# Choice of experts in a two-block transformer kernel: lists in their own place, ten U tiles kept back, more rows gathered early, angles at the end

## The chip, the cores and the metric

The kernel runs on one core of one Trainium2 chip. The metric is the device time of one launch in microseconds. Before the change the median of 3 runs is 2347.88 us (2346.62 to 2350.38).

## The reference

512 tokens of width 1024 go through two blocks. The part that the change touches is the feed-forward of the first block, a choice among 16384 experts (PEER). For each token, each of 8 heads scores two sets of 128 keys, takes the 16 best of each, adds them up in pairs, and takes the 16 best of the sums. These name 128 experts a token; expert i has a row of expert_u and a row of expert_v.

```
q = (xb @ w_q).reshape(p, PEER_HEADS, 2, PEER_DK_HALF)
sc = jnp.einsum('phcd,hcnd->phcn', q, sub_keys)
top_s, top_i = lax.top_k(sc, PEER_TOPK)
cand_s = top_s[:, :, 0, :, None] + top_s[:, :, 1, None, :]      # reshaped to (p, heads, 256)
cand_i = top_i[:, :, 0, :, None] * N_KEYS + top_i[:, :, 1, None, :]
best_s, best_pos = lax.top_k(cand_s, PEER_TOPK)
idx = jnp.take_along_axis(cand_i, best_pos, axis=-1)
g = jax.nn.softmax(best_s, axis=-1)
act = jax.nn.gelu(jnp.einsum('phkd,pd->phk', expert_u[idx], xb), approximate=False)
return jnp.einsum('phk,phkd->pd', g * act, expert_v[idx])
```

The second block (attention with rotary angles, then SwiGLU) needs cos and sin of the positions; they are computed inside the first block and put aside in DRAM (`csd`).

## The kernel before

The first block's mixer runs to about 245 us, PEER to about 1560, the second block to the end. Every fp32 weight is split in two parts, `whi` by ScalarE and `wlo` by VectorE or POOL (`split`, L91), and each product takes three matmuls.

Of the 512 tokens, 384 (three tiles) are done densely. All 16384 rows of expert_u are gone through as 128 tiles of U (`u_step(e)`, 24 matmuls and a Gelu each). The activations of the first 66 go to DRAM (`actd`), those of the next 22 stay in a ring. Their gates form a matrix G, built from one-hot tiles `oj`, `oi`, `oa` on VectorE (L813 to L816) and 48 product groups of 16 matmuls on TensorE (`pg`, L826 and L828), copied by ScalarE to `stage`, and written by SyncE to `gdram`. Then come 128 `v_step(e)`: read the activation, multiply by G (`cf`, L901), split (`ch`, `cl`), 18 matmuls with a tile of V. U steps 88 to 127 run beside V steps 66 to 105; this is called the middle stage. G comes in loads of eight steps (L899), U and V in blocks of two tiles (`raw`, L97), all through SyncE's queue.

The fourth tile of 128 tokens gathers: POOL fetches a row of expert_u for each token (`gather`, L641) and VectorE takes its dot product (L655, called a row), 128 times; then a Gelu, and 128 rows of expert_v, added up (L668). This tile is chosen first, so its rows can start early. `gs` is the generator of these steps.

`topk` (L482) is the choice for one tile on VectorE: MAX8, index and replace on 16 lists of 128 scores, then the candidates. The scores of the first tile are evicted during the w_q projection, those of the others go to DRAM (`scd`) and come back through SyncE.

What sets the order: `chain()` yields the VectorE work in pieces with a cost each, added to `now`. While `pe`, the work given to TensorE, is behind `now`, a U step is put in (4.2 each, 28 at the start); products are put in 9 after their one-hots; every 7 of cost a row. Within the v steps rows are spread by stage weights. A scheduler then fixes the order of each engine; each engine works in its order and waits where data is missing.

Of the kernel before, what the change touches and what calls it, by code (L numbers as in the profile page):

```python
# [18 lines left out]
P = 128  # L19
T = 512  # L20
# [6 lines left out]
U_PE = 4.2  # L27
G_PE = 1.8
LO_DVE = 1.25
ROW_DVE = 1.3  # L30
LAG = 9.0
U_LATE = 28.0
G_EVERY = 7.0
ROWS_AHEAD = 2
# [5 lines left out]
TB = 16  # L40
# [14 lines left out]
STARTS = [sum(ROWS[:a]) for a in range(16)]  # L55
# [13 lines left out]
class K:  # L69
# [412 lines left out]
    def topk(self, sc, tkp, consts, res, after_scores):  # L482


        nc = self.nc
        stc, wtc, btc = consts
        s1 = tkp.tile([P, 16, 16], F32, name="s1")
        ix = tkp.tile([P, 16, 16], U32, name="ix")
        for lo in (0, 8):
            for hc in range(16):  # L490
                nc.vector.max(s1[:, hc, lo:lo + 8], sc[:, hc])
                if hc % 4 == 3:
                    yield 1.1, True
            for hc in range(16):
                nc.vector.max_index(ix[:, hc, lo:lo + 8], s1[:, hc, lo:lo + 8], sc[:, hc])  # L495
                if hc % 4 == 3:
                    yield 1.4, True
            if lo == 0:
                for hc in range(16):
                    nc.vector.match_replace(out=sc[:, hc], in_to_replace=s1[:, hc, 0:8], in_values=sc[:, hc],  # L500
                                            imm_value=NEG)
                    if hc % 4 == 3:
                        yield 1.4, True
        after_scores()
# [11 lines left out]
        for lo in (0, 8):  # L516
            for h in range(8):
                nc.vector.max(bv[:, h, lo:lo + 8], cand[:, h])
            yield 1.5, True
            for h in range(8):  # L520
                nc.vector.max_index(bp[:, h, lo:lo + 8], bv[:, h, lo:lo + 8], cand[:, h])
            yield 2.1, True
            if lo == 0:
                for h in range(8):
                    nc.vector.match_replace(out=cand[:, h], in_to_replace=bv[:, h, 0:8], in_values=cand[:, h],
                                            imm_value=NEG)
                yield 2.1, False

# [57 lines left out]
    def peer(self):  # L586
# [3 lines left out]
        with ExitStack() as ctx:  # L590
# [54 lines left out]
            def gsteps():  # L645
                rows = []
                for k in range(P + ROWS_AHEAD):
# [28 lines left out]
            sctx = ctx.enter_context(ExitStack())  # L676
            scp = self.pool("sc", 1, ctx=sctx)

            def score_tile():
                return scp.tile([P, 16, P], F32, name="sc")  # L680

            order = list(reversed(range(T // P)))
            sc = [score_tile()]
            with ExitStack() as pctx:
# [32 lines left out]
                posi = tr[:, 0].bitcast(I32)  # L717
                nc.sync.dma_start(posi, a["pos"].to_broadcast([P, T]))
                nc.vector.tensor_copy(tr[:, 1], posi)
                hpi = kp.tile([P, 1], F32, name="hpi")  # L720
                nc.vector.memset(hpi, float(np.pi / 2))
# [9 lines left out]
            with ExitStack() as pctx:  # L731
                rp.append(self.pool("ring", 1, None, rctx, "right"))
                stgp = self.pool("stg", 2, ctx=pctx)
                ohp = self.pool("oh", 4, ctx=pctx)
                kp = self.pool("pk", 1, ctx=pctx)
                tkp = self.pool("tk", 1, ctx=pctx)
# [4 lines left out]
                stc = kp.tile([P, 16, 4], F16, name="stc")  # L741
                wtc = kp.tile([P, 16, 4], F16, name="wtc")
                btc = kp.tile([P, 16, 4], F16, name="btc")
                for r in range(16):
                    nc.gpsimd.memset(stc[:, r], float(STARTS[r]))
                    nc.gpsimd.memset(wtc[:, r], float(STARTS[r] - STARTS[r - 1]) if r else 0.0)
                    nc.gpsimd.memset(btc[:, r], float(r))
                io32 = kp.tile([P, P], I32, name="io32")
                nc.gpsimd.iota(io32, pattern=[[1, P]], base=0, channel_multiplier=0)
                iota4 = kp.tile([P, P, 4], F16, name="iota4")  # L750
                nc.vector.tensor_copy(iota4, io32[:, :, None].to_broadcast([P, P, 4]))
                consts = (stc, wtc, btc)

# [39 lines left out]
                def gates(tt):  # L793
# [13 lines left out]
                    for n in range(P // 8):  # L807
# [10 lines left out]
                        def products(n=n, oj=oj, oi=oi, oa=oa):  # L818
                            b, half = divmod(n, 2)
                            if half == 0:  # L820
                                stage[b] = stgp.tile([P, P, TB], F32, name="stage")
                            first = None
# [25 lines left out]
                self.early = -1  # L848
                dve = 0.0

                def pace(single):
                    while pe[0] < now[0] and todo:
                        u_step(todo.pop(0), nc.gpsimd if single else nc.vector)
                        pe[0] += U_PE
                        if not single:
                            now[0] += LO_DVE

                owed = [0.0]

                for cost, single in chain():  # L860
                    now[0] += cost
                    drain()
                    pace(single)
                    if self.early >= 0:
                        owed[0] += cost
                        while owed[0] > G_EVERY and self.early < P:
                            owed[0] -= G_EVERY
                            next(gs)
                            self.early += 1
                            now[0] += ROW_DVE  # L870
                while queue or todo:
                    now[0] += 1.0
                    drain(not todo)
                    pace(False)
                    owed[0] += 1.0
                    while owed[0] > G_EVERY and self.early < P:
                        owed[0] -= G_EVERY
                        next(gs)
                        self.early += 1
                        now[0] += ROW_DVE  # L880
            sctx.close()
# [684 lines left out]
```

## Time and profile before

| | us |
|---|---|
| median of 3 runs | 2347.88 |
| the profiled execution | 2345.79 |
| its span | 2344.0 |
| TensorE busy | 2204.4 (94%) |
| VectorE busy | 1652.3 (70%) |
| ScalarE busy | 921.5 (39%) |
| POOL busy | 533.9 (23%) |

The share of busy time is a mean over stages with different limits. In the chain of work that ended last TensorE has 75%, VectorE 14% and transfers 6%. A row of the trace gives start, duration, engine, line, operation, output and inputs, and in brackets how long the engine was idle before and what ended it. A time stretch of a window row is in us from the start of the span.

### The profile page before, as it was taken

Reading aid. Unit: us, or ns where it says so; the run is one execution under the profiler, and the core shown is the slowest. Engines: PE = TensorE matmul, PEld = TensorE weight load, DVE = VectorE, ACT = ScalarE, POOL = GpSimd, SP = SyncE. Lnnn points to the kernel's source line nnn. Section 1 sums busy time; section 2 is a strip of 40 time slices with the busy share of each in tenths; the row PEclk is TensorE's granted clock in tenths of the full one; section 3 lists DMA queues with packets and bytes.
Section 4 is the critical chain, followed back from the end, with each engine's and each line's share of the span. In section 5 each row is a group of like instructions: output and inputs, shape, how many; then the busy total and the mean of one; then the engine's idle time right before and its main releaser. Section 6 shows DMA issues by size and latency. Waiting matters only on the chain.

```text
span 2344.0 us, 29873 instructions
## 1 busy us (share of the span) xinstructions
PE 2204.4 (94%) x11063; PEld 1909.1 (81%) x11063; DVE 1652.3 (70%) x3113; ACT 921.5 (39%) x1345; POOL 533.9 (23%) x458
## 2 busy tenths in 40 slices
PE   4999989799999789999799999999999999999998
PEld 4888788699999768788688888878777888888887
DVE  8785679999777466778788887976666665444423
ACT  3623443246465423333233333354444554333321
POOL 3010022503300212333555554420112100000000
PEclk9989999999999989999899999999999999999999
DMA  7482344766766789999989998952221253322222
GB/s 277 147 283 75 135 170 165 256 220 249 251 231 223 268 280 314 324 314 336 330 319 345 345 351 323 320 169 100 81 69 55 97 173 117 108 90 96 82 91 74
DMA packets 158307, 483.66 MB, mean 206 GB/s; under 512 B 12232, under 2 KB 80456, under 8 KB 128080
## 3 DMA queue, kind: packets, MB, share of 16 engines
q1 hardware_dynamic: 116688, 330.73, 40.3%
q0 software_dynamic: 41472, 151.01, 18.2%
q8 instruction: 87, 1.43, 0.3%
q14 instruction: 60, 0.49, 0.1%
HBM read 429.65 MB, written 52.05 MB: 206 GB/s over the span
## 4 chain that ended last, share of the span: by engine, by line
PE 75%; DVE 14%; DMA 6%; issue 3%; ACT 1%; POOL 0%; SPq 0%; DVEq 0%; POOLq 0%; ACTq 0%
PE mm L115 12%; PE mm L117 12%; PE mm L118 12%; PE po L115 5%; PE act L118 5%; PE act L115 5%; PE act L117 5%; PE po L117 5%; PE po L118 5%; DMA sp<-actd 5%; DVE row L655 2%; PE pg L826 2%; PE pg L828 2%; DVE wlo L93 1%; DVE ix L495 1%
## 5 line engine op out<-in xcount | busy, mean ns | idle before, releaser
L93 DVE TENSOR_TENSOR wlo<-raw,whi 128x1024 fp32r<-128x1024 f32 (+1 forms) x380 | 454.4, 1201 | 260.4 <-ACT whi L92 256.1
L92 ACT ACTIVATE whi<-raw 128x1024 fp32r<-128x1024 f32 (+1 forms) x415 | 427.5, 1036 | 494.3 <-PE mm L117 196.1
L117 PE MATMUL mm<-hl,whi 128*128 128x512 f32 x928 | 368.9, 398 | 4.3 <-DVE hl L318 2.2
L115 PE MATMUL mm<-hh,whi 128*128 128x512 f32 x928 | 367.9, 400 | 4.5 <-ACT hh L471 1.6
L118 PE MATMUL act<-hh,wlo 128*128 128x384 f32 x1024 | 349.4, 342 | 17.0 <-DVE wlo L93 13.2
L118 PE MATMUL mm<-hh,wlo 128*128 128x512 f32 x928 | 363.8, 397 | 0.0
L115 PE MATMUL act<-hh,whi 128*128 128x384 f32 x1024 | 349.7, 342 | 2.7 <-ACT sp L612 2.7
L117 PE MATMUL act<-hl,whi 128*128 128x384 f32 x1024 | 348.5, 340 | 0.0
L115 PE MATMUL po<-whi,ch 128*128 128x512 f32 x768 | 268.6, 396 | 46.6 <-ACT ch L92 23.3
L117 PE MATMUL po<-wlo,ch 128*128 128x512 f32 x768 | 302.3, 394 | 4.4 <-DVE wlo L93 4.3
L118 PE MATMUL po<-whi,cl 128*128 128x512 f32 x768 | 296.1, 391 | 0.0
L641 POOL DMA_INDIRECT row<-in_eu_dram,gidx x128 | 171.2, 1337 | 531.6 <-DVE row L655 439.3
L641 POOL DMA_INDIRECT row<-in_ev_dram,gidx x128 | 184.4, 1441 | 184.9 <-DVE acc L668 146.8
L117 PEld LDWEIGHTS mm<-hl,whi 128*128 128x128 f32 x928 | 178.1, 192 | 43.0 <-DVE hl L972 3.0
L118 PEld LDWEIGHTS act<-hh,wlo 128*128 128x128 f32 x1024 | 195.2, 191 | 21.1 <-DVE wlo L93 15.6
L115 PEld LDWEIGHTS mm<-hh,whi 128*128 128x128 f32 x928 | 177.2, 192 | 42.6 <-ACT hh L471 2.0
L115 PEld LDWEIGHTS po<-whi,ch 128*128 128x128 f32 x768 | 145.4, 190 | 78.5 <-ACT whi L92 25.2
L118 PEld LDWEIGHTS mm<-hh,wlo 128*128 128x128 f32 x928 | 177.6, 191 | 37.1 <-DVE wlo L93 0.3
L115 PEld LDWEIGHTS act<-hh,whi 128*128 128x128 f32 x1024 | 195.7, 191 | 6.2 <-ACT sp L612 3.7
L117 PEld LDWEIGHTS act<-hl,whi 128*128 128x128 f32 x1024 | 195.6, 191 | 1.8
L92 ACT ACTIVATE ch<-cf 128x384 fp32r<-128x384 f32 x128 | 67.0, 525 | 325.1 <-PE po L117 167.1
L117 PEld LDWEIGHTS po<-wlo,ch 128*128 128x128 f32 x768 | 145.6, 190 | 36.2 <-DVE wlo L93 6.8
(476 smaller groups left out, 3444.3 us busy)
## 6 DMA issues: line engine op xcount, KB each, us to landing
raw<-in_uT_dram SPq DMA_DIRECT2D x64, 1024.0 KB
raw<-in_v_dram SPq DMA_DIRECT2D x64, 1024.0 KB
raw<-in_w_in_dram SPq DMA_DIRECT2D x26, 1024.0 KB
gdram<-stage SPq DMA_DIRECT2D x24, 1024.0 KB
G<-gdram SPq DMA_DIRECT2D x16, 1536.0 KB
raw<-in_w_gu_dram SPq DMA_DIRECT2D x22, 1024.0 KB
actd<-sp SPq DMA_DIRECT2D x66, 192.0 KB
sp<-actd SPq DMA_DIRECT2D x66, 192.0 KB
```

What stands on the lines that cost most here:

```text
L92: self.nc.scalar.activation(hi, src, AF.Copy)
L93: (eng or self.nc.vector).tensor_tensor(lo, src, hi.bitcast(F32), op=ALU.subtract)
L115: ins = nc.tensor.matmul(out, wh, xh, start=start and i == 0, stop=False)
L117: nc.tensor.matmul(out, wh, xl, start=False, stop=False)
L118: nc.tensor.matmul(out, wl, xh, start=False, stop=stop and i == n - 1)
L495: nc.vector.max_index(ix[:, hc, lo:lo + 8], s1[:, hc, lo:lo + 8], sc[:, hc])
L641: nc.gpsimd.indirect_dma_start(out=row, out_offset=None, in_=a[n], in_offset=bass.IndirectOffsetOnAxis(ap=gidx[:, k:k + 1], axis=0))
L655: ins = nc.vector.scalar_tensor_tensor(row, row, 1.0, self.h2g, op0=ALU.mult, op1=ALU.mult, accum_out=dots[:, n:n + 1])
L826: ins = nc.tensor.matmul(ps[:, t], oj[:, q, :, t], oa[:, q, :, t], start=True, stop=False)
L828: nc.tensor.matmul(ps[:, t], oj[:, q, :, t], oi[:, q, :, t], start=False, stop=True)
```

## The change

The planner's costs of the list pieces become smaller. The constants of the choice and its pool (`tk`) are made before the w_q projection, in a place that nothing else uses; the candidates, one-hots and lists of all tiles follow in the same pool. The angles (`trig`) and the store of `csd` move from behind the w_q projection to behind the last gates, with a tile of the `stage` pool. Of the 88 U steps, ten are kept back until the gates are all given out, and each of these gets two rows. Before, a row came every 7 of cost; now after two of three U steps. The Gelu between dots and second rows gets four empty steps on either side. Lines move by +1 up to about L660 and by a few behind it.

```
-G_EVERY = 7.0
+U_TAIL = 10
+DOTS = 8
...
                 if hc % 4 == 3:
-                    yield 1.1, True
+                    yield 0.85, True
...
-                nc.scalar.activation(dots, dots, AF.Gelu)
+                for _ in range(DOTS // 2):
+                    yield
+                tc.keep_in_program_order(nc.scalar.activation(dots, dots, AF.Gelu))
+                for _ in range(DOTS // 2):
+                    yield
...
             scp = self.pool("sc", 1, ctx=sctx)
+            tkp = self.pool("tk", 1, ctx=sctx)
...
+            stc = tkp.tile([P, 16, 4], F16, name="stc")
...
+            nc.vector.tensor_copy(iota4, io32[:, :, None].to_broadcast([P, P, 4]))
...
-                tr = stp.tile([P, 4, T], F32, name="tr", tag="scst")
...
-                self.trig(tr[:, 2], tr[:, 1], tr[:, 3], hpi)
-                nc.sync.dma_start(self.csd, tr[:, 2])
...
+                def row():
+                    if 0 <= self.early < P:
+                        next(gs)
+                        self.early += 1
+                        now[0] += ROW_DVE
+
+                def u_next(single):
+                    u_step(todo.pop(0), nc.gpsimd if single else nc.vector)
+                    pe[0] += U_PE
+                    if not single:
+                        now[0] += LO_DVE
 
                 for cost, single in chain():
                     now[0] += cost
                     drain()
-                    pace(single)
-                    if self.early >= 0:
-                        owed[0] += cost
-                        while owed[0] > G_EVERY and self.early < P:
...
+                    while pe[0] < now[0] and len(todo) > U_TAIL:
+                        u_next(single)
+                        if len(todo) % 3:
+                            row()
+                while todo:
+                    now[0] = max(now[0], pe[0])
+                    drain()
+                    u_next(False)
+                    for _ in range(2):
+                        row()
+                drain(True)
+
+                tr = stgp.tile([P, 4, T], F32, name="tr", tag="stage")
...
+                self.trig(tr[:, 2], tr[:, 1], tr[:, 3], hpi)
+                nc.sync.dma_start(self.csd, tr[:, 2])
...
-            left = 2 * P + ROWS_AHEAD - done
+            left = 2 * P + ROWS_AHEAD + DOTS - done
```

The first place is VectorE at the end of the w_q projection (`ql`: low half of a q block, evicted in this projection; `wlo`: low half of a weight; `s`, `ix`: the lists). Before:

```order
L93 TENSOR_TENSOR wlo<-raw,whi 128x1024
L93 TENSOR_TENSOR ql<-mm,qh 128x512
L93 TENSOR_TENSOR wlo<-raw,whi 128x1024 x2
L751 CAST iota_2172<-io_2170 128x512
L491 MAX s_2174<-sc 128x8 x16
L495 MAX_INDEX ix<-s_2174,sc 128x8 x16
L500 MATCH_REPLACE sc<-s_2174,sc 128x128 x16
L491 MAX s_2174<-sc 128x8 x16
L495 MAX_INDEX ix<-s_2174,sc 128x8 x16
```

After:

```order
L698 CAST iota_1716<-io_1714 128x512
L94 TENSOR_TENSOR wlo<-raw,whi 128x1024
L94 TENSOR_TENSOR ql<-mm,qh 128x512 x2
L492 MAX s_2147<-sc 128x8 x4
L496 MAX_INDEX ix<-s_2147,sc 128x8 x4
L501 MATCH_REPLACE sc<-s_2147,sc 128x128 x4
L492 MAX s_2147<-sc 128x8 x2
L94 TENSOR_TENSOR wlo<-raw,whi 128x1024
L492 MAX s_2147<-sc 128x8 x2
L496 MAX_INDEX ix<-s_2147,sc 128x8 x4
L94 TENSOR_TENSOR wlo<-raw,whi 128x1024
L94 TENSOR_TENSOR ql<-mm,qh 128x512 x2
```

The constant `iota` and three quarters of the first lists now stand among the evictions of the projection.

The second place is SyncE at the end of the gates. Before:

```order
L97 DMA raw<-in_v_dram 128x2048
L833 DMA gdram<-stage 128x2048
L97 DMA raw<-in_v_dram 128x2048 x2
L833 DMA gdram<-stage 128x2048 x2
L97 DMA raw<-in_v_dram 128x2048
L899 DMA G<-gdram 128x24x128 x2
L623 DMA sp<-actd 128x384 x2
```

After:

```order
L98 DMA raw<-in_v_dram 128x2048 x2
L827 DMA gdram<-stage 128x2048
L98 DMA raw<-in_v_dram 128x2048
L874 DMA tr<-in_pos_dram 128x512
L827 DMA gdram<-stage 128x2048
L98 DMA raw<-in_v_dram 128x2048
L879 DMA csd<-tr 128x512
L899 DMA G<-gdram 128x24x128 x2
L624 DMA sp<-actd 128x384 x2
```

The load of the positions, the store `csd` and their wait now stand ahead of the first load of G.

The third place is VectorE at the end of the gates. Before:

```order
L816 TENSOR_TENSOR oi<-oi,gt 128x1024
L93 TENSOR_TENSOR wlo<-raw,whi 128x1024
L816 TENSOR_TENSOR oi<-oi,gt 128x1024
L93 TENSOR_TENSOR wlo<-raw,whi 128x1024 x3
L901 TENSOR_TENSOR cf<-sp,G 128x384
L655 SCALAR_TENSOR_TENSOR row,dots<-row,h2g 128x1024
L901 TENSOR_TENSOR cf<-sp,G 128x384
```

After, from the last split ahead of the v steps on:

```order
L94 TENSOR_TENSOR wlo<-raw,whi 128x1024
L1003 TENSOR_SCALAR tr<-tr 64x512
L1005 SCALAR_TENSOR_TENSOR tr<-tr 64x512 x2
L656 SCALAR_TENSOR_TENSOR row,dots<-row,h2g 128x1024
L1005 SCALAR_TENSOR_TENSOR tr<-tr 64x512
L656 SCALAR_TENSOR_TENSOR row,dots<-row,h2g 128x1024
L1005 SCALAR_TENSOR_TENSOR tr<-tr 64x512
L656 SCALAR_TENSOR_TENSOR row,dots<-row,h2g 128x1024
L1002 TENSOR_SCALAR tr<-tr 64x512
L1003 TENSOR_SCALAR tr<-tr 64x512
L1005 SCALAR_TENSOR_TENSOR tr<-tr 64x512 x4
L1007 TENSOR_SCALAR tr<-tr 64x512
```

The angles and three rows stand behind the last split of this stage, ahead of the first cf.

## Rows read from the trace of the kernel before

**Rows 1.** Windows: stretch, length, busy us (instructions) per engine, TensorE clock, DMA share, GB/s.

```profile
294.00:508.00 214.00, 182.94 (x1016) 178.45 (x1015) 198.59 (x888) 73.03 (x101) 68.14 (x86) 0.94 0.57 195
508.00:808.00 300.00, 296.99 (x1942) 283.54 (x1939) 231.43 (x369) 166.43 (x199) 60.02 (x40) 1.00 0.69 244
810.00:825.00 15.00, 0.00 (x0) 0.00 (x0) 0.00 (x0) 0.00 (x0) 3.75 (x4) 0.57 0.99 333
850.00:1095.00 245.00, 240.59 (x1057) 197.47 (x1056) 181.21 (x271) 86.76 (x118) 68.78 (x46) 1.00 0.93 315
1095.00:1180.00 85.00, 69.34 (x334) 61.50 (x333) 65.96 (x104) 22.04 (x31) 49.36 (x33) 0.90 0.91 337
1097.00:1150.00 53.00, 51.01 (x252) 45.34 (x250) 52.08 (x83) 15.68 (x22) 41.92 (x27) 1.00 0.97 361
1180.00:1461.00 281.00, 273.38 (x1374) 247.00 (x1373) 239.04 (x239) 97.00 (x133) 149.04 (x104) 1.00 0.93 340
```

**Rows 2.** Timeline of ScalarE: start, us, instruction [idle before, what ended it].

```profile
485.26 1.06 ACT L92 ACTIVATE whi<-raw 128x1024 fp32r<-128x1024 f32 x1 [3.01 <-PE act L117]
489.42 1.06 ACT L92 ACTIVATE whi<-raw 128x1024 fp32r<-128x1024 f32 x1 [2.72 <-PE act L117]
...
1098.14 0.53 ACT L92 ACTIVATE ch<-cf 128x384 fp32r<-128x384 f32 x1 [2.60 <-issue]
1102.22 0.53 ACT L92 ACTIVATE ch<-cf 128x384 fp32r<-128x384 f32 x1 [2.60 <-issue]
```

**Rows 3.** Timelines of POOL, ScalarE, VectorE and SyncE, 298 to 335 us.

```profile
298.25 0.60 ACT L704 ACTIVATE sc<-scp 128x512 f32<-128x512 f32 x1 [3.29 <-PE scp L118]
...
308.33 0.10 POOL L745 MEMSET stc<- 128x4 f16 x1 [12.40 <-PE scp L118]
...
312.62 3.19 DVE L491 MAX8 s<-sc 128x8 f32<-128x128 f32 x16
...
331.49 0.32 SPq L776 DMA_DIRECT2D sc<-scd  x1
...
334.92 0.99 DVE L518 MAX8 bv<-cand 128x8 f32<-128x50 f32 x8
```

**Rows 4.** Tiles oi and pg: ns min/median/max, first and last start.

```profile
L816 DVE TENSOR_TENSOR oi<-oi,gt x48: 673/684/2878, 496.8 to 792.6; 128x1024 f16<-128x1024 f16 x48
L828 PE MATMUL pg<-oi,oj x384: 276/298/302, 507.5 to 802.2; 128*128 128x128 f16 x192
```

**Rows 5.** Groups of VectorE, 294 to 508 us: busy us, mean ns | idle before.

```profile
L93 DVE TENSOR_TENSOR wlo<-raw,whi 128x1024 fp32r<-128x1024 f32 x18 | 21.7, 1210 | 15.3 <-ACT whi L92 15.3
L655 DVE SCALAR_TENSOR_TENSOR row<-row,h2g 128x1024 f32<-128x1024 f32 x13 | 18.2, 1398 | 0.0
```

**Rows 6.** Timelines of ScalarE, SyncE and VectorE, 806 to 826 us.

```profile
806.93 1.06 ACT L92 ACTIVATE whi<-raw 128x1024 fp32r<-128x1024 f32 x1 [2.06 <-PE act L117]
...
810.57 5.04 SPq L899 DMA_DIRECT2D G<-gdram  x2
...
825.72 0.56 DVE L901 TENSOR_TENSOR cf<-sp,G 128x384 f32<-128x384 f32 x1 [16.47 <-DMA G<-gdram]
```

**Rows 7.** Tile tr, its waits, and the table load of ScalarE in its timeline.

```profile
L1005 DVE SCALAR_TENSOR_TENSOR tr<-tr x8: 689/689/690, 264.9 to 272.8; 64x512 f32<-64x512 f32 x8
L1003 DVE TENSOR_SCALAR tr<-tr x2: 424/424/425, 264.4 to 268.9; 64x512 f32<-64x512 f32 x2
...
L1010 ACT ACTIVATE tr<-tr,vec x1: 720/720/720, 277.2 to 277.2; 32x512 f32<-32x512 f32 x1
  DMA tr<-in_pos_dram: 4.9, 1
...
275.91 1.28 ACT L1010 ACT_TABLE_LOAD   x1
```

**Rows 8.** Timelines of SyncE and ScalarE, 1134 to 1166 us.

```profile
1134.09 17.19 SPq L97 DMA_DIRECT2D raw<-in_v_dram  x1
...
1162.56 2.95 ACT L92 ACTIVATE whi<-raw 128x1024 fp32r<-128x1024 f32 x3 [18.40 <-DMA raw<-in_v_dram]
```

More of the change, by code (lines that the diff above doesn't have):

```diff
@@ L496, in topk @@
                 if hc % 4 == 3:
-                    yield 1.4, True
+                    yield 1.1, True
             if lo == 0:
@@ L502, in topk @@
                     if hc % 4 == 3:
-                        yield 1.4, True
+                        yield 1.1, True
         after_scores()
@@ L518, in topk @@
                 nc.vector.max(bv[:, h, lo:lo + 8], cand[:, h])
-            yield 1.5, True
+            yield 1.4, True
             for h in range(8):
                 nc.vector.max_index(bp[:, h, lo:lo + 8], bv[:, h, lo:lo + 8], cand[:, h])
-            yield 2.1, True
+            yield 1.6, True
             if lo == 0:
@@ L526, in topk @@
                                             imm_value=NEG)
-                yield 2.1, False
+                yield 1.6, False
         e = tkp.tile([P, 16, 8], F32, name="e")
@@ L677, in peer @@
             scp = self.pool("sc", 1, ctx=sctx)
+            tkp = self.pool("tk", 1, ctx=sctx)
             def score_tile():
                 return scp.tile([P, 16, P], F32, name="sc")
+            stc = tkp.tile([P, 16, 4], F16, name="stc")
+            wtc = tkp.tile([P, 16, 4], F16, name="wtc")
+            btc = tkp.tile([P, 16, 4], F16, name="btc")
+            for r in range(16):
+                nc.gpsimd.memset(stc[:, r], float(STARTS[r]))
+                nc.gpsimd.memset(wtc[:, r], float(STARTS[r] - STARTS[r - 1]) if r else 0.0)
+                nc.gpsimd.memset(btc[:, r], float(r))
+            io32 = tkp.tile([P, P], I32, name="io32")
+            nc.gpsimd.iota(io32, pattern=[[1, P]], base=0, channel_multiplier=0)
+            iota4 = tkp.tile([P, P, 4], F16, name="iota4")
+            nc.vector.tensor_copy(iota4, io32[:, :, None].to_broadcast([P, P, 4]))
+            consts = (stc, wtc, btc)
             order = list(reversed(range(T // P)))
@@ L734, in peer @@
                 ohp = self.pool("oh", 4, ctx=pctx)
-                kp = self.pool("pk", 1, ctx=pctx)
-                tkp = self.pool("tk", 1, ctx=pctx)
                 pps = self.pool("pps", 2, PSUM, pctx)
@@ L739, in peer @@
                 pacts.append(self.pool("pact2", 1, PSUM, pctx))
[L741 to L752, printed above, removed]
                 now, pe = [0.0], [U_LATE]
@@ L820, in products @@
                             if half == 0:
-                                stage[b] = stgp.tile([P, P, TB], F32, name="stage")
+                                stage[b] = stgp.tile([P, P, TB], F32, name="stage", tag="stage")
                             first = None
@@ L848, in peer @@
                 self.early = -1
[L849 to L858, printed above, removed]
+                def row():
[8 more added lines that the diff above has]
+                        now[0] += LO_DVE
                 for cost, single in chain():
@@ L862, in peer @@
                     drain()
-                    pace(single)
-                    if self.early >= 0:
-                        owed[0] += cost
-                        while owed[0] > G_EVERY and self.early < P:
[L867 to L880, printed above, removed]
+                    while pe[0] < now[0] and len(todo) > U_TAIL:
[10 more added lines that the diff above has]
+                tr = stgp.tile([P, 4, T], F32, name="tr", tag="stage")
+                posi = tr[:, 0].bitcast(I32)
+                nc.sync.dma_start(posi, a["pos"].to_broadcast([P, T]))
+                nc.vector.tensor_copy(tr[:, 1], posi)
+                hpi = tkp.tile([P, 1], F32, name="hpi")
+                nc.vector.memset(hpi, float(np.pi / 2))
+                self.trig(tr[:, 2], tr[:, 1], tr[:, 3], hpi)
+                nc.sync.dma_start(self.csd, tr[:, 2])
             sctx.close()
```

5 lines of the change are left out of this document (removed).

## The prediction

> **What bounds the kernel now.** I read the windows by stage first, because a mean over the program hides the four stages that the change touches [rows 1]. From 508 to 808 us TensorE is busy 296.99 of 300 us at a granted clock of 1.00: it bounds that stage. From 294 to 508 it is busy 182.94 of 214 us and VectorE 198.59: the choice of experts on VectorE bounds that one. From 810 to 825 TensorE does nothing, and the clock falls to 0.57. From 1095 to 1180 it works 69.34 of 85 us, at 0.90, and from 1180 to 1461 it is back to 273.38 of 281. Then I read the ScalarE, VectorE and SyncE rows at the edges of these stages, to see what each waited for. The end of the kernel (the second block) follows the first on the same TensorE, so time saved ahead of it is saved at the end. One U step takes 489.42 - 485.26 = 4.16 us, one v step alone 1102.22 - 1098.14 = 4.08 [rows 2].
>
> Execution and runs: the profiled execution took 2345.79 us (span 2344.0), the median of the runs is 2347.88, 2.1 more. I make the sum against 2345.8 and add 2.1 at the end.
>
> **1. Lists in their own place, lower costs, ten kept-back U steps: the stage to 808.** Before, the POOL constants wait 12.40 us for TensorE to be done with the score matrices whose place they take (308.33), and VectorE's first MAX8 starts at 312.62, though the last quarter of the first tile's scores is written at 298.25 + 0.60 = 298.85. The candidates' first MAX8 is at 334.92 [rows 3], so list work of one tile takes 334.92 - 312.62 = 22.3 us. In the order after, three of the four quarters of the first lists stand between the evictions of the w_q projection, and only one quarter, 22.3 / 4 = 5.6 us, and some 2 us of candidate sums must follow 298.85. The candidates then come at 306.4, 28.5 us earlier. Those three quarters are about 17 us of VectorE work put into the w_q stage; VectorE also loses the angles there (8 x 0.69 and some eight short ones of 0.42, 9 us [rows 7]), and I take that stage as unchanged, from -2 to +2.
>
> Of the 28.5 us some is given back: ahead of the first product group the order after has 8 more rows and 3 more splits of U on VectorE, 8 x 1.40 + 3 x 1.21 = 14.8 us [rows 5]. The one-hot tile that ends the first group (L816, at 496.8 [rows 4]) so comes 13.7 us earlier, at 483. On TensorE the first product group started at 507.4, after 39.2 U steps; in the order after only 35.2 U steps stand before it. Before, TensorE was what it waited for: U steps follow one another without a gap in the 20 us ahead of it [rows 2]. Four steps less are 4 x 4.16 = 16.6 us, and of TensorE's 31 idle us in that window [rows 1] I take 6 away: a part of them follows the load of the second tile's scores, which SyncE issues at 331.49 when the first lists are done [rows 3], with blocks of U queued behind it; it now leaves earlier. I put the first group at 507.4 - 16.6 - 6 = 485. From there to the last U step the work is the 300 us of the second window, which TensorE fills, plus the four U steps, 316.6: the stage ends at 801.6 instead of 807.4 [rows 1, 4]. That is -6. Bounds: if the group keeps its 10.6 us behind L816 (507.4 - 496.8), it starts at 493.7 and the stage ends at 810.3, +3; with the kept-back steps delayed by their rows, +10. If all of the stall goes, -15.
>
> **2. Angles at the end of the gates.** Before, TensorE ends its last U step at 806.9 (the split's first half starts then), the last gate writes leave, the first load of G is issued at 810.57 and cf starts at 825.72, having waited 16.47 us for it [rows 6]. TensorE does nothing between 810 and 825, and the DMA engines are busy 0.99 [rows 1]: the load of 3.1 MB takes 15.1 us beside four gathers. After, the order puts the angle chain and three rows behind the second-to-last splits of VectorE (third place shown above), and the last split waits for ScalarE, which waits for the last U step. SyncE issues the first G only behind the csd store (second place), which waits for the sines, which wait for the chain. So from the end of U: 1.06 (whi) + 1.21 (wlo) + the chain behind it, 8 x 0.69 + 4 x 0.42 = 7.2, and three rows of 1.40, 4.2 [rows 5], together 11.4; then on ScalarE three of at most 0.72 and a table load of 1.28, 3.4 [rows 7]; then the landing of the store, 2.5 by my choice (between nothing and 4.9, what VectorE waited for the load of the positions [rows 7], and nearer to neither, so the middle). That is 19.6 us instead of the 3.6 of before (810.57 - 806.93): the issue moves 16 us. But with no gather beside it (POOL has run its rows while VectorE did the chain) 3.1 MB at the 333 GB/s of that window [rows 1] take 9.4 us, some 9.8 with its issue, instead of 15.1, which gives back 5.3. That is +10.7, and I take +10; bounds +5 (VectorE done with most of the chain while U still runs) and +16 (nothing given back). The angles' work in the w_q stage hid behind TensorE there, so taking it out gives nothing.
>
> **3. More rows early: the middle stage, e from 66 to 105.** A U step and a v step make 8.24 us. The whole stage takes 366 us (1095 to 1461, [rows 1]) against 40 x 8.24 = 329.6, 36 lost. Half of it stands in one place: a whi waits 18.40 us for a block of v [rows 8]. That block (issued at 1134.09, 17.19 us in SyncE's queue [rows 8]) shares the DMA engines with POOL's gathers, 27 of them from 1097 to 1150, while the rate is 361 GB/s at a share of 0.97 [rows 1].
>
> In the order after, 67 rows instead of 41 stand on VectorE before the first cf, 47 instead of 51 in the steps up to 66, and 113 instead of 132 in the middle stage. Bytes: 40 x (2 x 0.524 + 0.197) = 49.8 MB of U, V and G, and 0.524 MB a row: 119 MB before, 350 us at 340 GB/s, which is more than TensorE's 329.6; after, 109 MB, 321 us, which is less. So the stage changes its bound. Besides, after five steps the order after has four without a row (the empty steps around the Gelu), so POOL issues some 14 gathers and pauses where it issued 27. I take the 18 us as gone, and a quarter of the other 18: -22. Bounds 0 (the stall as it is) and -30.
>
> The 26 rows more ahead of 808 lie on VectorE, busy 231.43 of 300 us there [rows 1]: 26 x 1.40 = 36 us fit, and DMA is 0.69 busy. Four rows less in 850 to 1095, where TensorE is busy 240.59 of 245, give nothing.
>
> **Sum.** -6 + 10 - 22 = -18; 2345.8 - 18 = 2327.8, and with 2.1 for the median 2330.
>
> **A rule that speaks against step 3.** The trace shows the v block landing 28.4 us after its issue at 1134.09, whi at 1162.56 [rows 8]. The Trainium skill, "DMA: Bandwidth & Descriptors", section "Queues, rings and completion order", says that a DMA engine takes turns between the queues that have work, a packet each, and keeps order within one ring. By this rule SyncE's block waits whenever gathers are queued beside a load of G, however many bytes the stage has in all; the 28.4 us fit it. What that makes of the time is the first rival.
>
> **Rivals.** (a) The stall moves instead of going. From the step of 76 on the order after has 3.7 rows a step where it had 3.3, and a G load of 1.5 MB and a block of v of 1 MB still stand next to each other on SyncE every eight steps. For it: 0.93 DMA share in the whole stage [rows 1]. Against: from 1180 to 1461 the kernel before has gathers beside every G too, 104 of them, and TensorE is busy 273.38 of 281 [rows 1]. Then the middle gives -6 (a third of the stall) instead of -22: -6 + 10 - 6 = -2, 2346.
>
> (b) Slower: the ten kept-back steps are paced by their rows. Each carries two rows; there are three buffers, so a row's turn (issue, landing and 1.4 on VectorE) must be under 3 x 2.08 = 6.2 us, or U steps grow. It decides from there. For it: beside the load of G a transfer took 15.1 us, and VectorE has 1.21 + 2 x 1.40 = 4.0 of 4.16 us taken [rows 5]. Against: the stage has DMA to spare, 0.69. At a turn of 9 us a step takes 6.0 and ten lose 18; with the G load's full 16: -6 + 18 + 16 - 22 = +6, 2353.9.
>
> (c) All of it works: -15, +5 and -30, so 2308.
>
> **Chances.** Forecast 0.55, (a) 0.17, (b) 0.13, (c) 0.15. The forecast's own range is 2318 to 2342. The range for 8 in 10 takes in (a) and (c)'s greater part and just reaches (b)'s value: 2306 to 2354. 0.2%, 4.7 us, is about what a measurement of this kernel can tell from no change. Faster by more than that (under 2343.2): 0.52 of the forecast, (c), 0.04 of (a): 0.71. Within: 0.15. Slower: (b) and the rest, 0.14.
>
> **What would show it.** Step 1: the candidates' first MAX8 near 306, the first product group near 485, the last ring Gelu near 802. Step 2: the first load of G about 20 us after the end of the last U step, TensorE idle some 30 us there instead of 20. Step 3: no whi that waits over 5 us for a block of v between 66 and 105, and the stage near 344 us. Rival (a) shows as a wait of 10 us or more of whi at another step; (b) as last U steps that are more than 5 us apart, with VectorE waiting for row. The forecast is wrong if the first product group stays after 500, or if the middle stage keeps over 360 us.

## The result, and the profile after

The changed kernel takes 2319.26 us (median of 4 runs, 2316.84 to 2320.85) against 2347.25 before: a ratio of 0.988, interval 0.9862 to 0.9897, 28 us faster. The forecast was 2330, and the time lies in its range, near the faster end of the forecast's own (2318 to 2342). The profiled execution has a span of 2315.1 (before 2344.0).

Four marks split the difference. They are ScalarE's rows: the split behind the last U step, and ch of V steps 0, 66 and 106.

| mark | before | after | change in the stage that ends here |
|---|---|---|---|
| end of U | 806.93 | 793.98 | -12.95 |
| ch of step 0 | 826.31 | 825.92 | +12.56 |
| ch of step 66 | 1102.22 | 1098.87 | -2.96 |
| ch of step 106 | 1452.95 | 1426.87 | -22.73 |
| end of the span | 2344.0 | 2315.1 | -2.82 |

The last line is code that the change doesn't touch; over the kernels below, the stretch from ch 106 to the end was 888.2 to 891.7 us, so 3 us there is scatter.

Windows of the kernel after (columns as in [rows 1]):

```profile
294.00:480.00 186.00, 160.99 (x906) 158.33 (x905) 182.50 (x767) 66.26 (x91) 69.48 (x40) 0.95 0.66 223
480.00:794.00 314.00, 314.00 (x2043) 300.61 (x2042) 263.58 (x455) 172.67 (x206) 79.90 (x53) 1.00 0.76 268
794.00:828.00 34.00, 1.62 (x5) 1.21 (x5) 14.80 (x24) 5.73 (x8) 9.98 (x10) 0.55 0.87 280
1098.87:1426.87 328.00, 325.13 (x1633) 293.94 (x1632) 269.94 (x284) 115.18 (x159) 169.29 (x114) 1.00 0.91 332
```

and of the kernel before, to the end of U and in the middle stage, cut at the same marks:

```profile
294.00:480.00 186.00, 155.10 (x857) 151.54 (x856) 170.59 (x808) 60.44 (x84) 65.39 (x83) 0.93 0.56 195
480.00:807.00 327.00, 324.76 (x2100) 310.45 (x2098) 259.43 (x450) 178.02 (x213) 62.77 (x42) 1.00 0.68 239
1102.22:1452.95 350.73, 327.45 (x1633) 295.18 (x1632) 291.78 (x324) 114.11 (x157) 193.01 (x133) 0.98 0.93 341
```

TensorE fills all of 480 to 794, does nothing for most of 34 us, and then is busy 325.13 of 328.00 in the middle stage, where it was busy 327.45 of 350.73. The DMA rate there fell from 341 to 332 GB/s.

VectorE at the start of the choice, and the first and last product group on TensorE, in timeline and tile view (before in [rows 3, 4]):

```profile
298.86 0.87 DVE L492 MAX8 s<-sc 128x8 f32<-128x128 f32 x4 [3.40 <-ACT sc L723]
306.02 0.98 DVE L519 MAX8 bv<-cand 128x8 f32<-128x50 f32 x8
```

```profile
L820 PE MATMUL pg<-oa,oj x384: 284/297/303, 480.0 to 785.4; 128*128 128x128 f16 x192
```

The candidates come at 306.02 instead of 334.92, the first group at 480.0 instead of 507.4.

The boundary, timelines of ScalarE, VectorE and SyncE (before in [rows 6]):

```profile
793.98 1.06 ACT L93 ACTIVATE whi<-raw 128x1024 fp32r<-128x1024 f32 x1 [2.73 <-PE act L118]
...
795.07 1.23 DVE L94 TENSOR_TENSOR wlo<-raw,whi 128x1024 fp32r<-128x1024 f32 x1 [1.41 <-ACT whi L93]
807.27 0.42 DVE L1007 TENSOR_SCALAR tr<-tr 64x512 f32<-64x512 f32 x1
...
810.40 0.71 ACT L1011 ACTIVATE tr<-tr,hpi 32x512 f32<-32x512 f32 x1
...
811.14 0.33 SPq L879 DMA_DIRECT2D csd<-tr  x1
817.31 4.20 SPq L899 DMA_DIRECT2D G<-gdram  x2
...
825.33 0.56 DVE L901 TENSOR_TENSOR cf<-sp,G 128x384 f32<-128x384 f32 x1 [17.64 <-DMA G<-gdram]
```

One step hands over to the next here: the last split (795.07), the angle chain to 807.27, the sines to 811.1, the csd store at 811.14, the first load of G at 817.31, cf at 825.33. TensorE stands for 32 us where it stood for 19. What SyncE waited for there (us in total, times, longest), the transfers issued from 808 to 820 with their KB and us to landing, and what SyncE's hardware queue (q1) moved from 817 to 827 (packets, MB, share of the engines' time):

```profile
SPq L899 <- DMA csd<-tr: 5.7, 1, 5.7
...
G<-gdram SPq DMA_DIRECT2D x2, 1536.0 KB, 8.0
csd<-tr SPq DMA_DIRECT2D x1, 256.0 KB, 6.1
row<-in_eu_dram,gidx POOLq DMA_INDIRECT x4, 6.5
...
q1 hardware_dynamic: 4733, 2.42, 92.2%
```

G waits for nothing but the landing of csd, which runs beside four gathers. Two loads of G leave together, 1.57 MB each; the first holds steps 0 to 7, and cf of step 0 reads only that one. From 817 to 827 the queue moved 2.42 MB, so the second load had not landed when cf started at 825.33: the 8.0 us are those of 1.57 MB, not of 3.1.

### The profile page after: what moved, and what is told of

Its sections match the earlier page's. It is cut to its first block, busy times and chain, and to the rows that moved or that the text cites. A ratio compares the mean times of both kernels' runs of the same rounds, so it can differ in the third digit from the quotient of the medians.

```text
span 2315.1 us, 29877 instructions
## 1 busy us (share of the span) xinstructions
PE 2191.9 (95%) x11063; PEld 1901.6 (82%) x11063; DVE 1654.0 (71%) x3118; ACT 924.1 (40%) x1346; POOL 529.9 (23%) x453
## 4 chain that ended last, share of the span: by engine, by line
PE 79%; DVE 10%; issue 6%; DMA 2%; POOL 2%; ACT 2%; DVEq 0%; POOLq 0%; ACTq 0%; SPq 0%
PE mm L116 12%; PE mm L118 12%; PE mm L119 12%; PE act L119 6%; PE act L116 6%; PE act L118 6%; PE po L118 5%; PE po L119 5%; PE po L116 5%; PE pg L820 2%; PE pg L822 2%; POOL row L642 2%; DVE row L656 1%; DVE ix L496 1%; DMA sp<-actd 1%
## 5 line engine op out<-in xcount | busy, mean ns | idle before, releaser
L94 DVE TENSOR_TENSOR wlo<-raw,whi 128x1024 fp32r<-128x1024 f32 (+1 forms) x385 | 461.1, 1200 | 221.9 <-ACT whi L93 214.4
L116 PE MATMUL po<-whi,ch 128*128 128x512 f32 x768 | 281.5, 393 | 33.9 <-ACT ch L93 32.4
L642 POOL DMA_INDIRECT row<-in_ev_dram,gidx x128 | 189.3, 1479 | 197.2 <-DVE acc L673 145.0
```

The lines of the kernel that those rows point to most:

```text
L94: (eng or self.nc.vector).tensor_tensor(lo, src, hi.bitcast(F32), op=ALU.subtract)
L116: ins = nc.tensor.matmul(out, wh, xh, start=start and i == 0, stop=False)
L642: nc.gpsimd.indirect_dma_start(out=row, out_offset=None, in_=a[n], in_offset=bass.IndirectOffsetOnAxis(ap=gidx[:, k:k + 1], axis=0))
```

## The experiments

Of each kernel the same marks were read from its profiled execution. Rows ahead of cf 0 and in the middle stage are counted in VectorE's order. Time is the median.

| kernel | last pg starts | ch 0 | steps 0-66 | middle stage | rows early / middle | time |
|---|---|---|---|---|---|---|
| before | 802.1 | 826.3 | 275.9 | 350.7 | 41 / 132 | 2347.3 |
| after | 785.4 | 825.9 | 273.0 | 328.0 | 67 / 113 | 2319.3 |
| e1 | 787.1 | 811.0 | 276.0 | 328.1 | 66 / 113 | 2307.1 |
| e2 | 758.3 | 796.8 | 275.1 | 352.2 | 41 / 129 | 2316.4 |
| e3 | 785.0 | 826.1 | 271.3 | 328.0 | 67 / 116 | 2315.7 |
| e5 | 789.6 | 805.9 | 269.9 | 343.1 | 41 / 132 | 2321.1 |
| e6 | 792.4 | 815.8 | 264.9 | 327.5 | 67 / 113 | 2306.8 |
| e12 | 767.4 | 794.6 | 291.1 | 330.8 | 48 / 117 | 2306.4 |
| e14 | 809.2 | 843.0 | 271.1 | 328.4 | 66 / 114 | 2336.7 |
| e18 | 786.5 | 826.6 | 270.4 | 326.3 | 67 / 116 | 2316.7 |
| e20 | 778.8 | 801.2 | 277.4 | 340.5 | 54 / 121 | 2312.6 |
| e29 | 805.5 | 835.1 | 266.5 | 329.9 | 67 / 113 | 2324.6 |
| e30 | 823.1 | 846.4 | 275.0 | 331.6 | 66 / 117 | 2340.8 |
| e35 | 753.9 | 790.9 | 267.0 | 328.7 | 41 / 129 | 2278.6 |

Ratios to the kernel before: e1 0.9838 (0.9814 to 0.9863), e2 0.9879 (0.9857 to 0.9901), e5 0.9901 (0.9879 to 0.9924), e6 0.9836 (0.9818 to 0.9854), e12 0.9824 (0.9807 to 0.984), e14 0.9955 (0.9943 to 0.9967), e20 0.9861 (0.9826 to 0.9896), e29 0.9909 (0.9874 to 0.9944), e30 0.9981 (0.9965 to 0.9998).

**e1, angles back.** Edit to the changed kernel:

```
                 self.proj([a["w_q"][i] for i in range(4)], KT, hh, hl, qfn, pps, tag="pps")
+                tr = stp.tile([P, 4, T], F32, name="tr", tag="scst")
...
+                self.trig(tr[:, 2], tr[:, 1], tr[:, 3], hpi)
+                nc.sync.dma_start(self.csd, tr[:, 2])
```

> The changed kernel with the angles and the csd store back behind the w_q projection; all else as changed. My theory: the angle chain ahead of the first load of G costs what the changed kernel loses between the end of U and the first cf (31 us against 19, 12.6). Then the first load of G is issued within 4 us of the end of the last U step, the first cf starts about 813 instead of 825, and the time is 2319 - 12 = 2307. Rival: the 9 us of angle work on VectorE beside the first lists in the w_q projection delay the choice, so the first product group starts some 9 us later than 480 and the end of U moves by 5 to 9: 2312 to 2316. Second rival: the load of G is slowed by gathers again as it was before (15 us instead of 8): 2314.

Timelines of SyncE, ScalarE and VectorE of e1:

```profile
796.49 4.47 SPq L898 DMA_DIRECT2D G<-gdram  x2
...
810.98 0.99 ACT L93 ACTIVATE ch<-cf 128x384 fp32r<-128x384 f32 x2 [13.85 <-DVE cf L900]
...
807.69 1.23 DVE L656 SCALAR_TENSOR_TENSOR row<-row,h2g 128x1024 f32<-128x1024 f32 x1 [6.25 <-DMA row<-in_eu_dram,gidx]
...
810.39 1.02 DVE L900 TENSOR_TENSOR cf<-sp,G 128x384 f32<-128x384 f32 x2
```

G leaves at 796.49, right behind U, and ch 0 comes at 811 as expected: the angles cost the changed kernel 12 us of time and 15 at ch 0. In the w_q stage they cost about 2 (first group at 481.6). From G's issue to cf it is 14 us again, but cf does not wait for G at its turn: in VectorE's order it stands behind two rows, the first of which waits 6.25 us for its gather. So the second rival's 15 us is not a slower load here.

**e2, rows as before.**

```
-                    if 0 <= self.early < P:
+                    if 0 <= self.early < 43:
```

> The changed kernel, but the planner stops giving early rows at 43 steps (some 41 rows on VectorE ahead of the first cf, as before); the pause around the Gelu of the dots stays. My theory (fewer rows, so fewer bytes in the middle stage): the middle stage, 328 us from V step 66 to 106 in the changed kernel and 351 before, goes back to 345 to 352, and the time to about 2340. Rival (it is the pause around the Gelu, not the number of rows): the middle stage stays within 4 us of 328 and the time within 5 of 2319. The stage ahead of 808 is filled by TensorE and should not get shorter.

Tile pg, timelines and middle stage of e2:

```profile
L820 PE MATMUL pg<-oa,oj x384: 284/297/303, 481.3 to 758.3; 128*128 128x128 f16 x192
...
786.38 0.33 SPq L879 DMA_DIRECT2D csd<-tr  x1
788.43 4.03 SPq L899 DMA_DIRECT2D G<-gdram  x2
...
796.81 0.52 ACT L93 ACTIVATE ch<-cf 128x384 fp32r<-128x384 f32 x1 [4.88 <-DVE cf L901]
...
1071.88:1424.10 352.22, 329.16 (x1633) 295.99 (x1632) 286.43 (x318) 113.25 (x157) 184.34 (x130) 0.98 0.90 334
```

The middle stage did go back to 352, but the time did not move, which neither theory had. The gates end 27 us earlier, so nine U steps are left behind the last product group, where the changed kernel has three. They cover the write of the gates, the angles and part of G's load, and ch 0 stands 29 us earlier. Early rows were not free. The csd store, with no gather under way, lets G go after 2.05 us.

Where the price of the rows arises, the windows from the first to the last product group show, of the changed kernel and of e2:

```profile
480.00:785.50 305.50, 305.50 (x1995) 292.31 (x1995) 256.25 (x444) 169.61 (x201) 75.96 (x50) 1.00 0.76 268
481.30:758.50 277.20, 277.20 (x1836) 266.33 (x1835) 226.66 (x397) 159.02 (x188) 57.49 (x36) 1.00 0.71 251
```

TensorE is never idle in either. The changed kernel has 159 matmuls more there, 6.6 U steps of 24, and 6.6 x 4.16 = 27.6 us is nearly all of the 28.3 by which its stretch is longer. The planner adds each row's cost to `now` and then puts in U steps until `pe` has caught up, so early rows bring U steps ahead of the product groups in TensorE's order. VectorE's work does not hold up TensorE here; VectorE waits for it (20.2 us for pg in the changed kernel, 26.6 in e2).

**e3, no pause** (`DOTS = 0`).

> The changed kernel without the eight empty steps around the Gelu of the dots; the early rows stay. My theory: 19 rows fewer in the middle stage do the work, and without the pause it gets at most 6 us longer, 328 to 334; time 2319 to 2325. Rival (the pause): a stall of 10 us or more beside a load of G comes back, the middle stage is 340 to 350 and the time 2331 to 2341.

The middle stage is 328.0, so the empty steps do nothing to it; the time, 2315.7, lies 3 us under the expected range. The order still had three steps without rows around the Gelu, so e18 had to follow.

**e5, own place alone** (the kernel before, with the block of constants and `tkp` moved as in the change's diff).

> The kernel before with only the choice's pool and constants allocated ahead of the w_q projection, in their own place; planner's costs, rows, angles and steps as before. My theory: the first candidates come some 25 us earlier, and since the planner's U steps are unchanged, TensorE's idle time ahead of the first product group shrinks by 10 or so; the end of U moves from 807 to 795 to 800, the middle stall stays: 2336 to 2340. Rival: VectorE has the angles and first lists in the same stage, so the lists gain little (10 us or less) and the end of U moves under 4 us: 2343 to 2348.

Windows of e5:

```profile
294.00:480.00 186.00, 161.52 (x918) 159.32 (x916) 183.12 (x801) 64.56 (x90) 69.02 (x35) 0.94 0.59 206
480.00:795.00 315.00, 313.90 (x2044) 300.76 (x2042) 238.41 (x374) 174.95 (x209) 67.03 (x45) 1.00 0.70 252
```

The time is 15 us under what either theory had. The end of U is at 794.43, all of what the change gains there. Ch 0 gained 8 more than that: no gather was issued between 780 and 807 us, and cf came 9 us after G's issue where it had taken 15. The runs scatter from 2310 to 2325, and the profiled one is the fastest; the 343 of its middle stage may flatter it.

**e6, angles in the middle** (in the place of the scores, between two tiles' gates).

```
                     yield from gates(order[2])
+                    angles()
+                    yield 9.0, False
                     yield from gates(order[3])
```

> The changed kernel with the angles between the gates of the second and of the last tile, in the place of the scores, which is free by then. The angles at their old place gave 2307 and 15 us less at the first cf than the changed kernel. My theory (the chain ahead of G's load is what was lost): the same gain, first cf at 810 to 814, time 2305 to 2309; TensorE fills that stage, so the 9 us of angles on VectorE cost nothing. Rival (VectorE bounds the gates, as the kernel with 41 early rows suggests, whose gates end 27 us earlier): the angles push the last gates back by 9, the first cf comes at 819 or later and the time is 2313 or more.

```profile
L820 PE MATMUL pg<-oa,oj x384: 278/297/303, 478.2 to 792.4; 128*128 128x128 f16 x192
```

This row of tile pg has the last group at 792.4, 7 us later than after, as the rival had it, and ch 0 is at 816; still the time is that of e1. TensorE is busy 314.40 of 314.40 us from the first to the last group, with 48 matmuls (two U steps) more than after, so the gates are put back by the 9.0 in the planner's count rather than by VectorE's work. In its profiled execution the V steps lost nothing at their start (264.9), which made up for it.

**e12, rows behind the gates.** To e6:

```
-                            row()
+                            row(43)
...
+                        last[0] = nc.vector.tensor_tensor(oi, oi, bc(gt[:, 1]), op=ALU.mult)
...
+                coef[0] = last[0]
                 while todo:
```

> The last kernel (angles between gates), but only 43 steps of rows are given before the last one-hot; the kept-back U steps get two rows each, held behind the last one-hot on VectorE. My theory now: rows among the gates delay the gates on VectorE (last product group at 785 with 67 rows, at 758 with 41), and the gates' end decides when G can be loaded; rows behind them cost nothing. Expected: last product group near 768, first cf at 796 to 800, just behind the last U step, middle stage 328 to 331 as in the changed kernel: 2290 to 2295. Rival (gathers beside the write and load of G slow these, so nothing is won over the angles alone): first cf at 808 or later, 2303 or more.

Tile pg, ScalarE and the first 20 V steps of e12, and the same steps of e6:

```profile
L821 PE MATMUL pg<-oa,oj x384: 278/297/303, 482.1 to 767.4; 128*128 128x128 f16 x192
...
794.64 0.53 ACT L93 ACTIVATE ch<-cf 128x384 fp32r<-128x384 f32 x1 [1.38 <-DVE cf L906]
...
794.64:897.99 103.35, 86.65 (x357) 68.68 (x356) 75.32 (x117) 30.52 (x42) 37.20 (x29) 0.95 0.94 333
815.81:891.60 75.79, 75.22 (x325) 62.15 (x326) 59.01 (x90) 26.76 (x38) 22.66 (x16) 0.97 0.94 321
```

The first cf comes right behind U, as expected, but the time missed by 12: the first 20 V steps take 103 us where e6 took 76. DMA is equally busy, 0.94, in both, but e12 has 29 POOL instructions (gathers) there against 16, and 13 gathers of 0.524 MB are 20 us at 333 GB/s: what moved behind the gates was late behind U.

**e14, old costs.**

> The changed kernel with the planner's costs for the list pieces as before. In its order 45 U steps stand ahead of the first product group instead of 35. My theory: the end of U is set by TensorE's idle time ahead of the first group, which the own place of the lists cut, not the costs; the end of U stays within 4 us of 794, first group near 520, and the time within 6 of 2319. Rival (the lower costs free VectorE from splits early): the end of U moves back by 8 or more and the time to 2327 or more.

Tiles pg and oj of e14, and who waited for pg:

```profile
L820 PE MATMUL pg<-oa,oj x384: 273/297/304, 525.0 to 809.2; 128*128 128x128 f16 x192
L807 DVE TENSOR_TENSOR oj<-iota,it x48: 667/689/1906, 468.9 to 799.9; 128x1024 f16<-128x1024 f16 x48
  PE pg L822: 23.1, 19
```

My theory fell. The first one-hot is made at 468.9, but 45 U steps stand ahead of the first group on TensorE, which starts at 525.0, and the gates end 24 us later than after. The lower costs matter because they give TensorE the first group when VectorE has it. No U step is left behind the last group in e14, so nothing covers the write of the gates, the angles and the load of G, and ch 0 is at 843. How the lateness is carried through the 48 groups is not shown: VectorE's wait on pg, 23.1 us, is hardly longer than the 20.2 of after.

**e18, no Gelu between.**

> The changed kernel without the empty steps and without the Gelu and the gate factor between the dots and the second rows (this part of the computation is left out), so that the rows run on without the pause of three to five steps which even the kernel without empty steps had at its Gelu, just where G of step 72 is loaded. My theory (19 rows fewer in the middle stage bring its bytes under what TensorE needs): the middle stage stays at 328 to 334, time 2314 to 2324. Rival (the pause of the gathers beside that load of G): a step of over 15 us comes back near 72, middle stage 338 to 350, time 2327 to 2341.

Timelines of POOL and SyncE of e18 at the load of G that leaves at step 72 (it holds steps 80 to 87):

```profile
1121.05 1.30 POOL L642 DMA_INDIRECT row<-in_ev_dram,gidx  x1 [0.30 <-issue]
1122.95 0.94 POOL L642 DMA_INDIRECT row<-in_ev_dram,gidx  x1 [0.60 <-DVE row L656]
1126.38 1.01 POOL L642 DMA_INDIRECT row<-in_ev_dram,gidx  x1 [2.49 <-DVE acc L667]
1129.66 0.93 POOL L642 DMA_INDIRECT row<-in_ev_dram,gidx  x1 [2.26 <-DVE acc L667]
...
1121.57 0.38 SPq L893 DMA_DIRECT2D G<-gdram  x1
```

Gathers leave right beside that load, no whi waits over 4.5 us for a block of v, and the middle stage is 326.3. The pause is not the cause. The gathers are thinner there than before, though: 22 leave from 1097 to 1150, where the kernel before had 27.

**e29, old place.**

> The changed kernel with the choice's pool and constants back in the place that the w_q projection's tiles leave free; costs, rows, kept-back steps and angles as changed. My theory: the own place is what shortened TensorE's idle time ahead of the last U step (807 to 794 with it alone). Without it the first candidates come at 330 to 335 again, the end of U at 805 to 812, the first cf at 836 to 845, middle stage 328: time 2331 to 2338. Rival (rows and costs already fill that gap): end of U within 5 us of 794 and the time 2316 to 2324.

VectorE's first MAX8, tile pg and SyncE at the end of the gates of e29:

```profile
311.20 3.18 DVE L492 MAX8 s<-sc 128x8 f32<-128x128 f32 x16
...
L820 PE MATMUL pg<-oa,oj x384: 274/297/302, 510.9 to 805.5; 128*128 128x128 f16 x192
...
826.02 0.32 SPq L879 DMA_DIRECT2D csd<-tr  x1
826.44 4.59 SPq L899 DMA_DIRECT2D G<-gdram  x2
```

My theory missed: the end of U, 798.85, is within the rival's 5 us, and the time lies within 1 us of the rival's range. The gates end 20 us later than after, but the time rises by only 5. Ch 0 comes 9 us later, and the first V steps give 6 of that back. The own place is worth 25 us alone and 5 in this company, so the parts of the change overlap; which wait they share is not shown. SyncE's rows show one thing more: here G leaves 0.42 us behind csd, without waiting for its landing, so the wait of the changed kernel does not come from standing behind csd in one queue.

**e30, rows alone** (before, `G_EVERY = 4.2`).

> The kernel before with only a row every 4.2 of cost instead of 7, which puts 66 rows on VectorE ahead of the first cf instead of 41 and 117 in the middle stage instead of 132. My theory now: a row ahead of the first cf takes about as much from the end of the gates as it gives back in the middle stage, so the middle stage falls from 351 to 328 to 335, the first cf moves from 826 to 840 to 850, and the time stays at 2340 to 2352. Rival (my forecast's: early rows are free, since VectorE is busy 231 of 300 us there): the first cf stays within 5 us of 826 and the time falls to 2322 to 2331.

```profile
L826 PE MATMUL pg<-oa,oj x384: 272/297/302, 529.0 to 823.1; 128*128 128x128 f16 x192
...
846.38 0.52 ACT L92 ACTIVATE ch<-cf 128x384 fp32r<-128x384 f32 x1 [21.44 <-DVE cf L901]
...
1121.37:1452.98 331.61, 326.41 (x1633) 295.22 (x1632) 275.58 (x292) 114.34 (x157) 174.28 (x118) 0.99 0.92 335
```

Tile pg, ScalarE's ch 0 and the middle stage: 20 us later at ch 0, 19 us shorter in the middle, and ch 106 at 1452.98 against 1452.95 before. The time is 0.9981 of before. Here the first group is already late, at 529.0 against 507.4, and the gates take as long as before (294 us). Rows early pay for themselves and little more.

**e20, half the rows** (e6, stopped at 56).

> The kernel with the angles between the gates (2306.8), with rows stopped at 56 steps: 54 rows ahead of the first cf instead of 67, 121 in the middle stage instead of 113. My theory (rows pay for themselves): last product group some 12 us earlier, near 780, first cf near 803, middle stage 336 to 342, time 2302 to 2311, the same within its interval. Rival (the middle stage has a threshold and is at TensorE's own 328 with 121 rows too): the first cf is early and the middle stage stays at 328 to 331, so 2292 to 2298, the best so far.

```profile
1078.57:1419.06 340.49, 328.30 (x1633) 295.09 (x1632) 276.87 (x301) 112.91 (x157) 179.75 (x122) 0.99 0.90 333
```

The middle stage lies between, 340.5 with 121 rows. There is no threshold to gain from; the time came 2 us above the expected range.

**e35, half the bytes.** To e2:

```
+                nc.gpsimd.indirect_dma_start(out=row[:, :512], out_offset=None,
+                                             in_=a[n].rearrange("n (a b) -> (n a) b", b=512), ...
+                return row                       # VectorE uses row[:, :512] for both halves
```

> The kernel with 41 early rows (e2: middle stage 352 us, 2316), but each gather fetches only the first 512 columns of a row, which VectorE then uses for both halves (so the other half of each row is left out of the computation): the same number of gathers, of rows and of elements on VectorE, half the bytes, 129 x 0.262 = 34 MB instead of 68 in the middle stage. My theory (bytes): the middle stage falls to 327 to 331, TensorE's own, with 129 rows in it, and the time to 2285 to 2296. Rival (number of gathers and rows, through POOL or VectorE): the middle stage stays at 345 or more, and the time above 2306.

```profile
1057.88:1386.59 328.71, 325.49 (x1633) 295.17 (x1632) 288.39 (x380) 113.97 (x157) 189.11 (x131) 0.99 0.74 254
```

129 rows, 131 POOL instructions, and 328.71 us at 254 GB/s: with the bytes halved, the number of rows no longer matters. The time is 6 us under the expected range: ch 0 comes 6 us earlier than in e2, and steps 0 to 66 take 8 less.

## Why the prediction was right, and where it was not

**Step 1 (end of U, -6 forecast, -13 measured).** The place was right: candidates at 306.0 (forecast 306.4), first group at 480 (485). The size was not. The forecast took away 6 of TensorE's 31 idle us in the first window. From 294 to the end of U, idle time fell by about 8 (from 512.9 - 479.9 to 500.0 - 475.0). The other 5 are busy time: the records have 8 matmuls fewer, and the granted clock from 294 to 480 is 0.95 instead of 0.93; how much each gives is not shown. With the own place alone (e5) it is -12.5; the costs then are needed to keep that when more rows stand early (e14).

**Step 2 (boundary, +10 forecast, +12.6 measured).** The chain behind the last split and the three ScalarE operations took the times that were worked out (795.07 to 807.7, then 3.4). The csd store was mis-sized: 6.1 us to landing where I chose 2.5, since four gathers were still under way; in e2, with none, G leaves after 2.05. The load then took 8.0, not 9.8, which gave some back. That these are so near is luck: the 9.8 counted the 3.1 MB of two loads, and cf waits for the 1.57 MB of the first; the 15.1 us of before are those of this load beside four gathers. What was not seen is that the cost of the angles hangs on the rows: in e2, with the same angles, it is hidden behind nine U steps.

**Step 3 (middle stage, -22 forecast, -22.7 measured).** The cause holds: fewer bytes bring the stage down to TensorE's own time. e2, e20, e30 and e35 give 352, 340.5, 331.6 and 328.7 us for 68, 63, 61 and 34 MB of gathers; with 49.8 MB of U, V and G beside them, the first three are as long as their bytes at 333 to 335 GB/s (341 before, 348 in e5's fastest run), until TensorE's 328 is longer.

That the size fits so well is in part luck. The 366 us of the forecast, between round marks, are 15 more than the stage has (350.73), and of its 36 lost us only 23 were there (350.73 - 327.45); it took away 22 of 36, and the change took nearly all of 23. In each kernel that loses time here a large part stands in one wait of whi for a block of v, behind the load of G that leaves at step 72 (18.40 us before, 15.10 in e2, 12.63 in e5, 9.84 in e20). Whether the bytes of the whole stage set its length or their crowding at this place is not separated.

Rival (a) is out: the longest such wait of the changed kernel is 6.70 us, where its sign was 10 (two waits, 6.62 and 6.70, do miss the step's own sign of none over 5), and in e18 gathers and the load of G run side by side without a stall. The rule of the Trainium skill that was set against the step ("DMA: Bandwidth & Descriptors", "Queues, rings and completion order") says who takes turns, not how much there is to move, and here the bytes decided.

The sentence of step 3 that failed is "26 x 1.40 = 36 us fit". VectorE had the time, but its time was not the price. The planner counts each row and puts U steps in for it, so 26 rows put the gates back by 27 us on a TensorE that is never idle (e2 against after). G cannot be loaded before: without the late angles its first load is issued 7 to 12 us behind the last product group (e1, e5, e6, e12, e20). This took back all or nearly all that the middle stage won (e2 and after: 2316 and 2319; e30 and before: 2341 and 2345 in the same session). Rows that the planner doesn't count were not run. In e14, e29 and e30, where no U step is left behind the gates, TensorE does stand idle among them, for 5 to 11 us, so there VectorE or ScalarE has a share.

So the sum came out in range with one term too small by 7, one too small by 3 the other way, and 6 us (steps 0 to 66 and the end) that no step had. No single part carries the gain. The own place alone gives 25 us (e5), all the rest without it 20 (e29, 2344.8 to 2324.6 in one session), the change without the lower costs 10 (e14); the rows are worth 4 alone (e30) and nothing clear of noise with the other edits (e2), and the late angles cost 12 (e1). The lower costs alone were not run.

**Rival (b)** did not happen as told: the last U steps stayed 4.16 us apart. Its place was close, though: rows did delay something in that stage, the gates, by way of TensorE's order.

The best versions that compute everything are e1, e6 and e12, 2306 to 2307, equal within their intervals. A reading of why e12 wins nothing over e6: from the end of U on, bytes that aren't moved early have to be moved late. What might beat them is use of the DMA queues ahead of 480 us, where they are 0.66 busy; that was not tried, since VectorE is busy 182.50 of 186 us there. With `U_TAIL = 0` the program is the same as with 10, so it was not run, and keeping ten back has no share in the gain: the planner keeps that many steps back anyway. Why ch 0 to 66 differs by 10 us between kernels with the same rows (264.9 to 276.0) stays open.

## What to carry to other kernels

Before work is moved into another engine's spare time, ask what else in the schedule hangs on it: 26 rows fitted VectorE's idle time, yet the planner's count of them put U steps ahead of the gates on TensorE and delayed these by 27 us. Where a stage is as long as its bytes, count bytes at the stage's own rate (here 333 to 348 GB/s) and stop when the next limit is reached. A small store whose landing a large load waits for costs that landing, 6 us here beside gathers and 2 without; put it where nothing waits for it.

## What was unexpected of the hardware

A store of 0.26 MB took 6.1 us to land beside four gathers, about what one of these took (6.5), though a gather moves twice as much. With no gather under way, G left 2.05 us behind the same store (e2). The first load of G, 1.57 MB, had landed after 8.0 us with no gather issued beside it (8.9 in e5), and after 15.1 with four (before).
